# Splitting the squared keys for the norm: ScalarE squares twice and VectorE subtracts, instead of a ScalarE copy and a GpSimd subtraction

## The chip, the cores and the metric

The kernel runs on one core of one Trainium2 chip. The metric is the device time of one execution in microseconds (us), shown as the median of several runs. The profile's times are also in us; durations of single instructions are given in ns or us. The engines are TensorE (PE; its weight loads are listed as PEld), VectorE (DVE), ScalarE (ACT), GpSimd (POOL) and SyncE (SP), which issues nearly all DMAs. Each engine works through its own list of instructions in order.

## The reference

One layer of a hybrid trunk over 1024 tokens and 1024 channels: an input projection, an RWKV-7 branch and an HGRN2 branch, a gated merge, cross-attention into 256 memory tokens, a SwiGLU feed-forward, and a last RMSNorm. What the change touches is the normalisation of the RWKV-7 keys: each head (64 channels) of `k * k_k` is divided by its length.

```python
cols = cols + mu * (token_shift(cols) - cols)          # cols = rmsnorm(x) @ w_in
r, k, v, w_lo, a_lo, g_lo = jnp.split(cols, RW_SPLITS, axis=-1)
...
kk = heads(k * k_k)
kk = kk * lax.rsqrt(jnp.maximum(jnp.sum(kk * kk, axis=-1, keepdims=True), 1e-24))
k_mod = heads(k * (1 + (a - 1) * k_a))
```

## The kernel before

All matrix products of this stage run in a rounded float32 format (F32R). Where the full precision of float32 is wanted, an operand is split into `hi`, the value rounded to F32R, and `lo`, the remainder `src - hi`, also in F32R. Products are then sums over the parts: `mm3` adds three matmuls (hi·hi, hi·lo, lo·hi). The helper `split` makes the two parts: by default ScalarE copies `src` to `hi` (L283), then GpSimd subtracts (L287).

The stage around the change is `rw_prep`, from about 30 to 375 us of the span. It works feature-major: a tile `j` is 128 of the 1024 channels, and each tile has two halves `h` of 512 tokens. For each `j` it projects three columns of `w_in`, in the order k, r, v, each for both halves: 24 matmuls of 128x512 into a PSUM tile `pproj` (8 blocks of the contraction, three matmuls each). `shifted` then mixes each result with the one of the token before (ScalarE writes `mshift` at L439, VectorE finishes `k`, `r` or `v` at L442). The weights come as two DMAs of 256 KB per column (`wraw`); each half is split into `whi` (ScalarE) and `wlo` (GpSimd for the first half, VectorE for the second).

`factors(j, h)` is the rest, a generator that the loop steps between the projections. Its chain for one half is:

- ScalarE squares the scaled keys into `sq` (L510); `split` makes `sqh` and `sql` from it (L511, seen in the profile as L283 and L287).
- PE makes two products `pza` (L518, L519), ScalarE their sigmoids `sg` and `aa`, VectorE the running sum `cum` (L522), ScalarE the exponentials `E` and `En`.
- PE sums the squares over each head: two matmuls `pq` with the block matrix `hsum`, first on `sqh`, then on `sql` (L533).
- VectorE takes the maximum and the reciprocal of `pq` into `d` (L535, L536), and makes `ka` (L541), the products `AR` (L545) and `BK` (L555, L557, two of each, 64 rows at a time) and `rb` (L561). GpSimd makes another part of `AR` (L542), `t` (L549) and `km` (L550, L551).
- PE sums `rb` per head into `pb` (L565) and transposes `v` into `pv` (L570); VectorE copies `pb` to `bon` (L567) and makes `VZ` (L577), GpSimd adds a bias to it (L579). DMAs store `ar_d`, `bk_d`, `v_d` and `z_d`.

The order on each engine isn't written out in the code. The tile framework schedules this stage when the kernel is built, by costs and priorities of its own, so a change of one instruction moves others on every engine's list. The framework also adds the waits. The planner `Pace`, which the next stage uses, takes no part here.

Of the kernel before, what the change touches and what calls it, by code (L numbers as in the profile page):

```python
# [10 lines left out]
F32 = mybir.dt.float32  # L11
F32R = mybir.dt.float32r
AF = mybir.ActivationFunctionType
ALU = mybir.AluOpType
# [170 lines left out]
def tile_trunk(ctx, tc, x, mem, norm_mix_g, w_in, rw_mu, rw_w0, rw_w2, rw_a0, rw_a2, rw_g2,  # L185
# [3 lines left out]
    nc = tc.nc  # L189
# [76 lines left out]
    def vc(name, i=0):  # L266
        if name == "mix":
            return GM[:, i:i + 1]
        return VC[:, VI[name] + i:VI[name] + i + 1]
# [10 lines left out]
    def split(hi, lo, src, hi_eng="act", lo_eng="pool"):  # L280

        if hi_eng == "act":
            nc.scalar.activation(hi, src, AF.Copy)  # L283
        else:
            nc.vector.tensor_copy(hi, src)
        e = nc.gpsimd if lo_eng == "pool" else nc.vector
        e.tensor_tensor(lo, src, hi.bitcast(F32), op=ALU.subtract)  # L287
# [136 lines left out]
    def rw_prep(rctx):  # L424
# [79 lines left out]
        def factors(j, h):  # L504
            (ks, rs, vs), w2h, w2l, lnb = tiles[j]
            sl = slice(h * HALF, (h + 1) * HALF)
            k, r, v = ks[h], rs[h], vs[h]
            T = lambda name: fp.tile([P, HALF], F32, tag="tmp", name=name, bufs=10)
            sq = T("sq")
            nc.scalar.activation(sq, k, AF.Square, scale=vc("kk", j))  # L510
            sqs = [fp.tile([P, HALF], F32R, tag="tmp", name=n, bufs=10) for n in ("sqh", "sql")]  # L511
            split(*sqs, sq)

            sg, aa = T("sg"), T("aa")
            for n, (dst, bias) in enumerate(((sg, "w0"), (aa, "a0"))):
# [122 lines left out]
        for j in range(D // P):  # L638
            if j:
                inputs = tile_inputs(j)  # L640
                next(inputs)
            last()
            next(inputs)
            last()
            for h in range(NHALF):
                f = factors(j, h)
                next(f)
                next(inputs)
                with tc.issue_after(next(f)):
                    next(consts, None)  # L650
                next(inputs)
                pending.append(f)
# [1680 lines left out]
```

## Time and profile before

| | |
|---|---|
| median of 3 runs | 2314.49 us (2312.69 to 2317.57) |
| profiled execution | 2314.19 us, its span 2312.5 us |
| PE busy | 2269.3 us (98%) |
| DVE busy | 1575.7 us (68%) |
| ACT busy | 1142.2 us (49%) |
| POOL busy | 1061.6 us (46%) |
| mean granted TensorE clock | 0.996 |

The span runs from the first to the last instruction; the profiled execution is 1.7 us longer than that. A view by windows gives for each stretch the busy time of each engine with the number of instructions in brackets, the granted clock of TensorE (1.00 is full speed), the busy share of the DMA engines and their GB/s. A view in order of time gives for each row the start, the duration, the engine, the line, the operation, output<-inputs, the shape, the count, and in square brackets the idle time before the row with what ended it. Ends of matmuls are modelled and overlap: in a row of 128x512 matmuls each is shown with 0.39 us, while they start every 0.227 us.

### The profile page before, as it was taken

Reading aid. Unit: us, or ns where it says so; the run is one execution under the profiler, and the core shown is the slowest. Engines: PE = TensorE matmul, PEld = TensorE weight load, DVE = VectorE, ACT = ScalarE, POOL = GpSimd, SP = SyncE. Lnnn points to the kernel's source line nnn. Section 1 sums busy time; section 2 is a strip of 40 time slices with the busy share of each in tenths; the row PEclk is TensorE's granted clock in tenths of the full one; section 3 lists DMA queues with packets and bytes.
Section 4 is the critical chain, followed back from the end, with each engine's and each line's share of the span. In section 5 each row is a group of like instructions: output and inputs, shape, how many; then the busy total and the mean of one; then the engine's idle time right before and its main releaser. Section 6 shows DMA issues by size and latency. Waiting matters only on the chain.

```text
span 2312.5 us, 47099 instructions
## 1 busy us (share of the span) xinstructions
PE 2269.3 (98%) x18262; PEld 1863.3 (81%) x18262; DVE 1575.7 (68%) x2513; ACT 1142.2 (49%) x2275; POOL 1061.6 (46%) x1145
## 2 busy tenths in 40 slices
PE   7999999999999999999999999999999999999998
PEld 5788887777888887888788888888888888888887
DVE  5888984666777657777666566655778665566655
ACT  6546464556565655654666424443552333334433
POOL 3656664555565555666566200000266655551212
PEclk9999999999999999999999999999999999999999
DMA  5444555343334244534334897117933423348653
GB/s 174 113 127 121 136 131 165 72 104 76 87 108 126 75 117 108 141 83 112 89 89 129 277 355 259 60 56 256 289 125 119 131 91 115 96 160 308 201 172 120
DMA packets 393691, 327.94 MB, mean 142 GB/s; under 512 B 107595, under 2 KB 318653, under 8 KB 392061
## 3 DMA queue, kind: packets, MB, share of 16 engines
q1 hardware_dynamic: 391549, 319.17, 45.6%
q0 software_dynamic: 1344, 4.72, 0.5%
q8 instruction: 144, 2.36, 0.4%
q10 hardware_dynamic: 576, 1.05, 0.1%
q14 instruction: 78, 0.64, 0.1%
HBM read 228.12 MB, written 96.21 MB: 140 GB/s over the span
## 4 chain that ended last, share of the span: by engine, by line
PE 72%; DVE 4%; DMA 3%; issue 2%; ACT 1%; POOL 1%; SPq 0%; ACTq 0%; POOLq 0%; DVEq 0%
PE pproj L103 22%; PE P L302 6%; PE P L303 6%; PE P L301 6%; PE pw L303 3%; PE pw L302 2%; PE pw L301 2%; PE cm L103 2%; PE psA L103 2%; PE psc L103 1%; PE po L103 1%; PE acc L302 1%; PE pq L303 1%; PE pq L302 1%; PE pq L301 1%
## 5 line engine op out<-in xcount | busy, mean ns | idle before, releaser
L103 PE MATMUL pproj<-uh,whi 128*128 128x512 f32 x768 | 320.1, 417 | 1.2 <-DVE q L103 0.7
L103 PE MATMUL pproj<-uh,wlo 128*128 128x512 f32 x768 | 300.9, 392 | 2.9 <-POOL wlo L103 2.3
L103 PE MATMUL pproj<-ul,whi 128*128 128x512 f32 x768 | 301.4, 392 | 0.0
L287 POOL TENSOR_TENSOR wl<-wraw,wh 128x512 fp32r<-128x512 f32 x87 | 122.4, 1416 | 201.2 <-ACT wh L283 153.6
L103 POOL TENSOR_TENSOR wlo<-wraw,whi 128x512 fp32r<-128x512 f32 x96 | 128.9, 1354 | 122.1 <-ACT whi L103 116.5
L301 PE MATMUL pproj<-uh,whi 128*128 128x512 f32 (+1 forms) x432 | 172.2, 399 | 0.9 <-ACT uh L329 0.7
L303 PE MATMUL pproj<-uh,wlo 128*128 128x512 f32 (+1 forms) x432 | 170.8, 395 | 2.0 <-POOL wlo L287 2.0
L103 PEld LDWEIGHTS pproj<-uh,whi 128*128 128x128 f32 x768 | 144.5, 188 | 34.0 <-DVE q L103 2.0
L302 PE MATMUL pproj<-ul,whi 128*128 128x512 f32 (+1 forms) x432 | 171.0, 396 | 0.0
L103 PEld LDWEIGHTS pproj<-ul,whi 128*128 128x128 f32 x768 | 144.4, 188 | 32.3
L283 ACT ACTIVATE whi<-wraw 128x512 fp32r<-128x512 f32 (+1 forms) x166 | 101.6, 617 | 136.4 <-PE pw L303 71.5
L103 PEld LDWEIGHTS pproj<-uh,wlo 128*128 128x128 f32 x768 | 145.0, 189 | 28.7 <-POOL wlo L103 2.7
L278 POOL TENSOR_TENSOR ss<-ss,nhalf 128x4 f32<-128x4 f32 (+1 forms) x7 | 6.2, 881 | 322.9 <-DMA wraw<-in_xa_wo_dram 186.7
L287 POOL TENSOR_TENSOR wlT<-wraw,whT 128x512 fp32r<-128x512 f32 x72 | 103.1, 1440 | 81.3 <-ACT whT L283 58.9
L287 DVE TENSOR_TENSOR wlo<-wraw,whi 128x512 fp32r<-128x512 f32 x134 | 93.1, 700 | 55.1 <-ACT whi L283 53.1
L283 ACT ACTIVATE wh<-wraw 128x512 fp32r<-128x512 f32 x143 | 86.9, 623 | 88.4 <-PE P L302 65.5
L103 ACT ACT_TABLE_LOAD x90 | 115.5, 1283 | 13.5 <-DVE m L103 6.4
L302 PE MATMUL acc<-wl,th 128*128 128x512 f32 x308 | 119.9, 389 | 0.2 <-DVE wl L287 0.2
L301 PE MATMUL acc<-wh,th 128*128 128x512 f32 x308 | 119.8, 389 | 0.0
L303 PE MATMUL acc<-wh,tl 128*128 128x512 f32 x308 | 119.8, 389 | 0.0
L2277 DVE TENSOR_TENSOR tl<-tl,th 128x512 fp32r<-128x512 f32 x77 | 60.1, 795 | 62.6 <-ACT th L2276 61.3
L301 PE MATMUL pw<-whi,ah 128*128 128x512 f32 x256 | 100.7, 393 | 0.9 <-ACT ah L283 0.6
(461 smaller groups left out, 6436.3 us busy)
## 6 DMA issues: line engine op xcount, KB each, us to landing
wraw<-in_w_in_dram SPq DMA_DIRECT2D x148, 256.0 KB
wraw<-in_ffn_w_dram SPq DMA_DIRECT2D x145, 256.0 KB
y<-in_ffn_w_dram SPq DMA_DIRECT2D x22, 512.0 KB
wsum_d<-y SPq DMA_DIRECT2D x11, 1024.0 KB
hsum_d<-s SPq DMA_DIRECT2D x44, 256.0 KB
tl<-hsum_d SPq DMA_DIRECT2D x44, 256.0 KB
wraw<-wsum_d SPq DMA_DIRECT2D x44, 256.0 KB
hid_d<-s SPq DMA_DIRECT2D x33, 256.0 KB
```

The source lines that it names most:

```text
L103: r = getattr(self.engine, op)(*a, **kw)
L278: nc.gpsimd.tensor_tensor(dst, tmp, nhalf[:, 0:n], op=ALU.pow)
L283: nc.scalar.activation(hi, src, AF.Copy)
L287: e.tensor_tensor(lo, src, hi.bitcast(F32), op=ALU.subtract)
L301: nc.tensor.matmul(ps, ah, bh, start=first, stop=False)
L302: nc.tensor.matmul(ps, ah, bl, start=False, stop=False)
L303: nc.tensor.matmul(ps, al, bh, start=False, stop=last)
L2277: tt(hl, hl.bitcast(F32), hh.bitcast(F32), op=ALU.subtract)
```

## The change

`sqh` no longer is a copy of `sq`: ScalarE squares the scaled keys a second time, straight into the F32R tile. The remainder `sql` is subtracted on VectorE instead of GpSimd. Per half this is one ScalarE instruction in place of another, one instruction less on GpSimd and one more on VectorE; there are 16 halves.

```diff
@@ -509,7 +509,8 @@
             sq = T("sq")
             nc.scalar.activation(sq, k, AF.Square, scale=vc("kk", j))
             sqs = [fp.tile([P, HALF], F32R, tag="tmp", name=n, bufs=10) for n in ("sqh", "sql")]
-            split(*sqs, sq)
+            nc.scalar.activation(sqs[0], k, AF.Square, scale=vc("kk", j))
+            nc.vector.tensor_tensor(sqs[1], sq, sqs[0].bitcast(F32), op=ALU.subtract)
```

Since the diff adds a line, lines from L512 on have a number higher by one in the changed kernel. The scheduler gives other orders in `rw_prep`. The first place is VectorE in a tile of the middle, j = 5 (j = 2 to 6 read alike here): the second half of the work of h = 0 up to `d` of h = 1 (`d_2612`). Before:

```order
L557 TENSOR_TENSOR BK<-km,En 64x8x64
L561 SCALAR_TENSOR_TENSOR rb<-r,VC,km 128x512
L442 SCALAR_TENSOR_TENSOR r<-pproj,VD,mshift 128x512
L522 SCALAR_TENSOR_TENSOR cum<-rst_120,sg 128x512
L287 TENSOR_TENSOR wlo<-wraw,whi 128x512
L535 TENSOR_SCALAR d_2612<-pq 128x512
```

Now:

```order
L558 TENSOR_TENSOR BK<-km,En 64x8x64
L562 SCALAR_TENSOR_TENSOR rb<-r,VC,km 128x512
L442 SCALAR_TENSOR_TENSOR r<-pproj,VD,mshift 128x512
L513 TENSOR_TENSOR sql<-sq,sqh 128x512
L287 TENSOR_TENSOR wlo<-wraw,whi 128x512
L523 SCALAR_TENSOR_TENSOR cum<-rst_120,sg 128x512
L442 SCALAR_TENSOR_TENSOR v<-pproj,VD,mshift 128x512
L536 TENSOR_SCALAR d_2612<-pq 128x512
```

`sql` of h = 1 stands behind `rb` of h = 0 and `r` of h = 1; `cum` and `wlo` have changed places, and a `v` has moved ahead of `d` (before, it stood behind the reciprocal that follows `d`, and a second `v` behind the next `rb`, where there is none now).

The second place is GpSimd at the end of h = 1 of the same tile and the start of the next, where `sql` of the next tile's h = 0 stood. Before:

```order
L579 TENSOR_TENSOR VZ<-VZ,lnb 128x512
L287 TENSOR_TENSOR sql<-sq,sqh 128x512
L287 TENSOR_TENSOR wlo<-wraw,whi 128x512
L579 TENSOR_TENSOR VZ<-VZ,lnb 128x512
L528 COPY eLall<-E 128x8
```

Now:

```order
L580 TENSOR_TENSOR VZ<-VZ,lnb 128x512
L287 TENSOR_TENSOR wlo<-wraw,whi 128x512
L580 TENSOR_TENSOR VZ<-VZ,lnb 128x512
L529 COPY eLall<-E 128x8
```

Only `sql` is gone there; in the half h = 0 it is gone from between `km` and the memset of `E` in the same way.

The third place is VectorE where that `sql` went, at the start of the next tile (j = 6, h = 0). Now:

```order
L568 COPY bon<-pb 128x8
L578 TENSOR_TENSOR VZ<-pv,bon 128x512
L513 TENSOR_TENSOR sql<-sq,sqh 128x512
L568 COPY bon<-pb 128x8
L442 SCALAR_TENSOR_TENSOR k<-pproj,VD,mshift 128x512
```

It stands between the `VZ` of h = 0 and the `bon` of h = 1; the rows around it are as before. On PE the two matmuls `pq` stand at the same place as before, one behind the other, in every half but the second of the first tile: there nine matmuls of a projection now stand between the one on `sqh` and the one on `sql`.

Three more moves are small. In the last tile VectorE's subtraction for `g2s` (L673) has moved from ahead of `ka` of h = 0 to behind `sql` of h = 1, and GpSimd's for `g2l` from ahead of its part of `AR` (L542) to behind it. On ScalarE in the tiles 2 to 6 the second `whi` of a column has moved ahead of the table load for `sg`, and a `mshift` ahead of the one for `E`. On SP the first of two weight loads at a tile's end has moved behind the stores `v_d` and `z_d` of h = 1.

## The prediction

> **What bounds the kernel.** I read the page first, then the waits of TensorE in the stage that the change touches, then that stage in order of time, engine by engine.
>
> ```profile
> PE 2269.3 (98%) x18262; PEld 1863.3 (81%) x18262; DVE 1575.7 (68%) x2513; ACT 1142.2 (49%) x2275; POOL 1061.6 (46%) x1145
> 50.00:375.00 325.00, 317.02 (x1464) 261.61 (x1464) 278.18 (x291) 174.82 (x263) 197.82 (x265) 0.98 0.48 130
> ```
>
> The first row is the page's busy times, the second the window of the stage: PE is busy for 317.0 of 325 us, so PE sets the time there too, and an instruction on another engine costs only where PE waits for it. VectorE is the next engine: 278.2 of 325 us (86%), against 198 on GpSimd and 175 on ScalarE. The change puts work on the fuller of the two engines. What PE waited for between 40 and 375 us (total, times, longest):
>
> ```profile
> PE pb L565 <- DVE bon L567: 3.0, 3, 1.4
> PE pq L533 <- POOL sql L287: 2.9, 1, 2.9
> ...
> PE pv L570 <- DVE v L442: 0.5, 1, 0.5
> ```
>
> So before the change `sql` makes PE wait once, in the first tile, for 2.9 us. In the other 15 halves it is early. The question is whether it is early on VectorE.
>
> **The prices of the instructions.** Groups of one shape in the stage (count, busy us, mean ns):
>
> ```profile
> L287 POOL TENSOR_TENSOR sql<-sq,sqh 128x512 fp32r<-128x512 f32 x16 | 21.8, 1361 | 0.5 <-POOL low L287 0.4
> L287 DVE TENSOR_TENSOR wlo<-wraw,whi 128x512 fp32r<-128x512 f32 x23 | 15.8, 687 | 0.0
> L510 ACT ACTIVATE sq<-k,VC 128x512 f32<-128x512 f32 x16 | 11.5, 717 | 33.4 <-DVE k L442 33.4
> L283 ACT ACTIVATE sqh<-sq 128x512 fp32r<-128x512 f32 x16 | 10.0, 626 | 0.3
> ```
>
> GpSimd loses 16 x 1.36 = 21.8 us. VectorE gains 16 subtractions; the same subtraction of the same shape, `wlo`, takes 0.69 us there, so 11.0 us. ScalarE pays 16 x (0.717 - 0.626) = 1.5 us. None of these three sums lies on the path by itself: ScalarE waits 33.4 us for `k` ahead of the same squares, and that idle time covers the 1.5 us. SP's moved weight load leaves only behind three small stores that were behind it, and its reader on ScalarE has its turn about a quarter of a tile later; if that cover is gone, `whi` is late and with it a projection. I cost both at nothing.
>
> **Where the new instruction is late.** PE in tile 5 (start, duration): the second `pq` of h = 0 and that of h = 1:
>
> ```profile
> 259.01 0.39 PE L533 MATMUL pq<-sql,hsum 128*128 128x512 f32 x1
> ...
> 271.29 0.39 PE L533 MATMUL pq<-sql,hsum 128*128 128x512 f32 x1
> ```
>
> Between the two halves PE has 12.28 us of work that waits for nothing. On VectorE the chain of h = 0 starts with the first of these and must reach `sql` of h = 1 by the last, since `sql` now stands behind `rb` and `r`:
>
> ```profile
> 259.44 0.69 DVE L535 TENSOR_SCALAR d<-pq 128x512 f32<-128x512 f32 x1 [0.89 <-PE pq L533]
> ...
> 264.85 1.78 DVE L555 SCALAR_TENSOR_TENSOR BK<-k,VC,t 64x512 f32<-64x512 f32 x1
> 266.55 2.56 DVE L545 TENSOR_TENSOR AR<-ka,E 64x512 f32<-64x512 f32 x2
> 269.14 0.68 DVE L557 TENSOR_TENSOR BK<-km,En 64x512 f32<-64x512 f32 x1
> 269.84 1.69 DVE L555 SCALAR_TENSOR_TENSOR BK<-k,VC,t 64x512 f32<-64x512 f32 x1
> 271.46 0.95 DVE L557 TENSOR_TENSOR BK<-km,En 64x512 f32<-64x512 f32 x1
> 272.44 0.84 DVE L561 SCALAR_TENSOR_TENSOR rb<-r,VC,km 128x512 f32<-128x512 f32 x1
> 273.20 0.74 DVE L442 SCALAR_TENSOR_TENSOR r<-pproj,VD,mshift 128x512 f32<-128x512 f32 x1
> 273.87 1.21 DVE L522 TENSOR_TENSOR_SCAN cum<-rst,sg 128x512 f32<-128x512 bf16 x1
> ```
>
> The rows left out are `r`, the reciprocal and `ka`. VectorE is never idle in it; from the first `pq` it is a chain of 15 us. In the old times `sql` would start where `cum` does, at 273.87, and end at 273.87 + 0.69 = 274.56, which is 3.27 us after PE asked for it. (The old `sql` was done on GpSimd at 266.57 + 1.28 = 267.85, the first row of the next fence.) PE works in order, so behind the waiting `pq` stand the 24 matmuls of `v` and all that follows.
>
> Part of the lateness goes with the change itself. GpSimd at the same time:
>
> ```profile
> 266.57 1.28 POOL L287 TENSOR_TENSOR sql<-sq,sqh 128x512 fp32r<-128x512 f32 x1
> 269.17 0.12 POOL L524 MEMSET E<- 128x8 f32 x1 [1.33 <-DVE AR L545]
> 269.27 1.72 POOL L287 TENSOR_TENSOR wlo<-wraw,whi 128x512 fp32r<-128x512 f32 x1
> 270.95 1.78 POOL L485 TENSOR_TENSOR w2l<-w2r,w2h 64x128 fp32r<-64x128 f32 x2
> ```
>
> and VectorE in the half h = 1, where GpSimd is silent:
>
> ```profile
> 283.29 1.40 DVE L545 TENSOR_TENSOR AR<-ka,E 64x512 f32<-64x512 f32 x2
> ...
> 285.42 0.75 DVE L555 SCALAR_TENSOR_TENSOR BK<-k,VC,t 64x512 f32<-64x512 f32 x1
> ```
>
> The pair L545 takes 1.40 us there and 2.56 beside the old `sql`: the two engines' subtractions and products exclude each other, and the one that comes second waits. With `sql` gone the pair ends 1.16 us earlier. But GpSimd's memset of `E` waits for that pair, and behind it stand `wlo` and `w2l`, whose inputs are there; they come earlier too and again hold up L555 (1.69 against 0.75 in the last row), L557 and `rb`. Played through with these durations, and each instruction held until the other engine's ends, `rb` ends near 272.3 instead of 273.28, so 0.95 of the 1.16 us is kept. I take a wait of 3.27 - 0.95 = 2.3 us. Bounds: with nothing kept 3.3; with all of 1.16 kept and the two later collisions (0.94 for L555, 0.26 + 0.09 for L557 and `rb`) gone as well, 3.27 - 2.45 = 0.8. I take 2.3 as nearest to the rows, since nothing removes `wlo`. Tiles 1 to 6 have the same PE distance and nearly the same chain, so 6 x 2.3 = 13.8 us.
>
> `sql` of h = 0 has its turn while VectorE waits for `mshift` and `sg`, well ahead of its `pq`: nothing. In the first tile `sql` of h = 1 falls behind `rb`. That wait is there already (2.9 us), and PE now does nine matmuls of it first; by the same collisions I make it 0.3 us longer in all.
>
> The last tile has its own rows:
>
> ```profile
> 342.26 0.77 DVE L673 TENSOR_TENSOR g2s<-g2r,g2s 32x512 fp32r<-32x512 f32 x1
> 352.32 1.21 DVE L522 TENSOR_TENSOR_SCAN cum<-rst,sg 128x512 f32<-128x512 bf16 x1
> ...
> 347.91 0.39 PE L533 MATMUL pq<-sql,hsum 128*128 128x512 f32 x1
> ```
>
> There `sql` would end at 352.32 + 0.69 = 353.0, 5.1 us after PE's turn. L673 (0.77) has moved behind it, and GpSimd's window loses `sql` (1.74 there) but gains `g2l` (1.30): 5.1 - 0.8 - 0.4 = 3.9 us. Bounds 4.3 and, with all of 1.74 kept, 2.6.
>
> **The clock after a wait.** What a wait of 1 to 3 us does to TensorE's granted clock (the column ahead of the last two):
>
> ```profile
> 134.49 1.05 PE L565 MATMUL pb<-hsum,rb 128*128 128x2 f32 x8 [1.30 <-DVE bon L567]
> 75.00:76.50 1.50, 1.50 (x4) 1.21 (x5) 1.49 (x3) 0.00 (x0) 1.44 (x4) 0.50 0.77 175
> 134.50:139.50 5.00, 5.00 (x21) 4.24 (x22) 2.31 (x5) 4.94 (x8) 4.22 (x5) 0.66 0.52 126
> 370.00:375.00 5.00, 4.37 (x12) 2.55 (x11) 1.22 (x2) 2.23 (x4) 4.02 (x5) 0.52 0.83 192
> 463.66 1.00 PE L103 MATMUL cm<-Z,AR 128*64 128x64 f32 x15 [1.66 <-DVE Z L103]
> 463.00:465.00 2.00, 1.29 (x32) 1.15 (x32) 1.79 (x6) 1.42 (x6) 1.32 (x3) 1.00 0.30 33
> ```
>
> After the waits of 2.9, 1.3 and 1.4 us the clock fell to half; after 1.66 us at 463 it did not. In the second window 5.0 x 0.34 / 0.5 = 3.4 us ran at half speed, which loses 1.7 us. I take three in four, so 1.28 us for each new wait: 7 x 1.28 = 9.0 us. [...]
>
> **What goes away.** PE comes to `pb` later, so VectorE's `bon` is ready: 3.0 us of waits, and the 0.5 for `v`, which now stands earlier. Of the `bon` waits two (1.30 and 1.44) were followed by half clock, 2 x 1.7 = 3.4. Together 6.9 us, at the ends of tiles 1, 5 and 7.
>
> **The sum.** 13.8 + 3.9 + 0.3 + 9.0 - 6.9 = +20.1 us. Against the profiled execution's 2314.2 that is 2334.3; the median of the runs is 0.3 above the profiled one, so 2334.6, and I say 2335. (A difference of 0.2%, 4.6 us, is about what a measurement of this kernel tells from none.)
>
> **Rivals.**
> 1. The waits come, but the clock stays up behind them, as it did at 463 us: 20.1 - 9.0 = +11.1, 2325.6. For it: that one wait. Against it: the other three. [...]
> 2. The waits are small, 0.8 us. That needs `wlo` and `w2l` to miss VectorE's gaps. Then 6 x 0.8 + 2.6 + 0.3 - 6.9, and a lost clock in the last tile alone, 1.3: +2.1, 2316.6, no difference. For it: all of `sql`'s 1.16 us comes back. Against it: the rows of `wlo` and `w2l`, which only come earlier.
> 3. Faster: freed of GpSimd, the chain fits between the two `pq`. From `pq` at 259.01 to the end of a `sql` it is 274.56 - 259.01 = 15.55 us; without any collision 1.03 less for the first L555 and 2.45 less for the rest, 12.07, under PE's 12.28. It decides from 3.27 us saved. Then only the removals count, with 0.8 left in the last tile: 0.3 + 0.8 - 6.9 = -5.8, 2308.7. Against it: the first L555 (1.78) meets GpSimd's `km`, not `sql`, and that stays.
>
> **How the numbers follow.** Forecast 0.57, rival 1 0.23, rival 2 0.14, rival 3 0.06. The predicted time is the forecast's, 2335. With nothing kept of the 1.16, seven drops of 1.7 us and 4.3 in the last tile it is 19.6 + 4.3 + 0.3 + 11.9 - 6.9 = +29.2, 2343.7: the upper end is 2344. At the lower end I leave out rival 3 and about the lower half of rival 2: 2317. The forecast and rival 1, with the upper part of rival 2, are slower by over 0.2%: 0.82; within: 0.12; faster: 0.06.
>
> **What would show it.** In the waits of PE: `pq` on VectorE's `sql`, eight times, some 2.3 us each in tiles 1 to 6 and 4 in the last, where there was one on GpSimd; the waits of `pb` on `bon` gone; windows of half clock behind most of the new waits; the pair L545 of h = 0 at 1.40 us; the distance from tile to tile up from 38.3 to some 41.5 us; the time from 375 us on unchanged. I am wrong if `sql` of h = 1 ends by the time of its `pq`, if the clock holds at 1.00 behind waits of 2 us, or if the time is given back after the stage.

## The result and the profile after

The changed kernel takes 2333.71 us (median of 5 runs, 2331.25 to 2335.66), the kernel before 2313.85 us in the runs beside it. The ratio is 1.0083, with a 95% interval of 1.0069 to 1.0098: 19.9 us slower. The prediction said 2335. The profiled execution of the changed kernel took 2335.24 us, with a span of 2333.2.

In the changed kernel `sql` is L513, `pq` L534, `AR` L546 and `rb` L562. What PE waited for between 40 and 400 us (total, times, longest), and the window of the stage in the same form as before (PE, its weight loads, VectorE, ScalarE, GpSimd; then granted clock, DMA share, GB/s):

```profile
PE pq L534 <- DVE sql L513: 19.1, 8, 3.5
...
50.00:375.00 325.00, 304.62 (x1381) 250.60 (x1380) 275.34 (x293) 167.55 (x246) 177.71 (x233) 0.97 0.45 122
```

One wait on GpSimd's `sql` has become eight on VectorE's. The waits on `bon` and `v` are gone; the two rows left out are waits for other tiles, at the start of the stage. PE is busy 12.4 us less in the same 325 us, although VectorE is no fuller than it was (275.3 us for 278.2; the same window now holds some 16 us less of the stage's work). That points to the place of the instruction rather than to VectorE's total, and the experiments test it. The eight waits, tile by tile (start, duration, and in brackets the idle time ahead):

```profile
77.87 0.50 PE L534 MATMUL pq<-sql,hsum 128*128 128x512 f32 x1 [3.21 <-DVE sql L513]
119.24 0.50 PE L534 MATMUL pq<-sql,hsum 128*128 128x512 f32 x1 [3.35 <-DVE sql L513]
161.05 0.51 PE L534 MATMUL pq<-sql,hsum 128*128 128x512 f32 x1 [1.88 <-DVE sql L513]
201.32 0.54 PE L534 MATMUL pq<-sql,hsum 128*128 128x512 f32 x1 [1.88 <-DVE sql L513]
243.16 0.50 PE L534 MATMUL pq<-sql,hsum 128*128 128x512 f32 x1 [1.88 <-DVE sql L513]
283.40 0.66 PE L534 MATMUL pq<-sql,hsum 128*128 128x512 f32 x1 [1.88 <-DVE sql L513]
324.91 0.50 PE L534 MATMUL pq<-sql,hsum 128*128 128x512 f32 x1 [1.53 <-DVE sql L513]
366.81 0.79 PE L534 MATMUL pq<-sql,hsum 128*128 128x512 f32 x1 [3.51 <-DVE sql L513]
```

VectorE in tile 5, from the `pq` of h = 0 to the `sql` of h = 1, and GpSimd's `wlo` beside it:

```profile
269.51 0.69 DVE L536 TENSOR_SCALAR d<-pq 128x512 f32<-128x512 f32 x1 [2.15 <-PE pq L534]
...
276.53 1.40 DVE L546 TENSOR_TENSOR AR<-ka,E 64x512 f32<-64x512 f32 x2
277.95 0.68 DVE L558 TENSOR_TENSOR BK<-km,En 64x512 f32<-64x512 f32 x1
278.65 1.69 DVE L556 SCALAR_TENSOR_TENSOR BK<-k,VC,t 64x512 f32<-64x512 f32 x1
280.26 0.95 DVE L558 TENSOR_TENSOR BK<-km,En 64x512 f32<-64x512 f32 x1
281.25 0.84 DVE L562 SCALAR_TENSOR_TENSOR rb<-r,VC,km 128x512 f32<-128x512 f32 x1
...
282.67 0.68 DVE L513 TENSOR_TENSOR sql<-sq,sqh 128x512 fp32r<-128x512 f32 x1
278.16 1.63 POOL L287 TENSOR_TENSOR wlo<-wraw,whi 128x512 fp32r<-128x512 f32 x1
```

`sql` ends at 283.35, and PE goes on at 283.40. The pair of `AR` is at 1.40 us, as forecast, and what follows it has the lengths it had before (1.69, 0.95, 0.84), only earlier. The granted clock (the column ahead of the last two) in the 5 us behind the four equal waits of tiles 2 to 5:

```profile
161.00:166.00 5.00, 4.95 (x22) 1.00 0.54 143
201.30:206.30 5.00, 4.98 (x15) 0.66 0.54 142
243.10:248.10 5.00, 4.94 (x22) 1.00 0.53 143
283.40:288.40 5.00, 5.00 (x15) 0.66 0.43 113
```

Two of the four were followed by half clock. What that costs can be read from the starts above: 201.32 - 161.05 = 40.27 and 283.40 - 243.16 = 40.24 us without, 243.16 - 201.32 = 41.84 us with it, so 1.6 us each. (In the kernel before, these steps from tile 2 to tile 5 took 38.2 to 38.3 us.) Half clock followed also in tiles 0, 1 and 7 (0.66, 0.66 and 0.50), and not in tile 6.

Where the loss stands along the span: starts of the same PE instructions after, less before, in us (median of those within 25 us from the time given in the kernel before, for the first profile of the changed kernel, its second profile (e10) and the experiments e2, e5, e7 and e8 below):

```
from    changed  again    e2     e5     e7     e8
 160      4.7     4.3    5.1    5.8    4.9   -2.1
 280     13.4    11.3   13.9   12.9   10.4   -2.8
 400     16.3    13.3   17.4   16.8    9.9   -5.2
 880     19.0    16.7   20.9   19.5   13.9   -5.0
1680     17.5    16.5   20.0   17.3   22.1   -4.2
2240     21.2    20.2   19.5   17.1   22.7   -3.7
```

So 16.3 of the 21.2 us of this execution were lost in the stage that was changed, and some 5 behind it. Most of these 5 come between 1680 and 2240 us, at one wait for `hB` at the start of the feed-forward part, with half clock behind it (0.50 from 1727.42 to 1730.82); the kernel before waits 0.5 us for `hB`:

```profile
1727.07 0.52 PE L301 MATMUL P<-hB,wh 128*128 128x512 f32 x1 [2.76 <-ACT hB L2026]
```

### The profile page after: what moved, and what is told of

It is laid out like the page before. It is cut to its first block, busy times and chain, and to the rows that moved or that the text cites. A ratio compares the mean times of both kernels' runs of the same rounds, so it can differ in the third digit from the quotient of the medians.

```text
span 2333.2 us, 47083 instructions
## 1 busy us (share of the span) xinstructions
PE 2274.2 (97%) x18262; PEld 1866.8 (80%) x18262; DVE 1582.6 (68%) x2529; ACT 1144.7 (49%) x2275; POOL 1055.9 (45%) x1129
## 4 chain that ended last, share of the span: by engine, by line
PE 76%; DVE 3%; DMA 2%; POOL 1%; issue 1%; ACT 1%; SPq 0%; ACTq 0%; POOLq 0%; DVEq 0%
PE pproj L103 21%; PE P L302 6%; PE P L303 6%; PE P L301 6%; PE acc L303 3%; PE acc L302 3%; PE acc L301 3%; PE pw L303 2%; PE pw L302 2%; PE pw L301 2%; PE cm L103 2%; PE psA L103 2%; PE psc L103 1%; PE po L103 1%; PE pq L303 1%; PE pq L302 1%
```

## Experiments: which part of the change costs

The theory: `sql` of h = 1 is late because it stands behind `rb` and `r` on VectorE. Rival A: the second Square on ScalarE is at fault. Rival B: VectorE is simply fuller, and each of the 16 subtractions costs the same. Four kernels take the change apart.

**e1, the ScalarE part alone.** Kernel before, with

```diff
-            split(*sqs, sq)
+            nc.scalar.activation(sqs[0], k, AF.Square, scale=vc("kk", j))
+            nc.gpsimd.tensor_tensor(sqs[1], sq, sqs[0].bitcast(F32), op=ALU.subtract)
```

> The ScalarE part of the change alone: `sqh` comes from a second Square, `sql` stays on GpSimd. Theory (the loss comes from where `sql` of h = 1 stands in VectorE's order, behind `rb` and `r`): as the kernel before, 2314 us, 2311 to 2317; PE waits at `pq` for GpSimd's `sql` in the first tile alone (about 2.9 us), and for `bon` three times (3.0 us). Rival A (the second Square: 0.72 us for 0.63, read from `k`, on ScalarE, makes `sqh` and what stands behind it late): slower, by up to the whole 20 us.

Measured: 2315.23 us, ratio to the kernel before 1.0005 (0.9996 to 1.0014). The stage's waits are those of before:

```profile
PE pb L566 <- DVE bon L568: 3.0, 3, 1.4
PE pq L534 <- POOL sql L513: 2.9, 1, 2.9
```

**e2, the VectorE part alone.** `split(*sqs, sq, lo_eng="dve")`: the copy on ScalarE stays, the subtraction goes to VectorE.

> The VectorE part of the change alone: `sqh` stays a copy of `sq` on ScalarE, `sql` comes from VectorE in both halves. Theory: as the changed kernel, 2334 us, 2330 to 2337, with eight waits of `pq` on VectorE's `sql`, 1.5 to 3.5 us each, 19 us together, and the waits on `bon` gone. Rival A (the second Square is at fault): back at 2314.

Measured: 2332.63 us, 1.0079 (1.0065 to 1.0093), with the eight waits:

```profile
PE pq L533 <- DVE sql L287: 20.0, 8, 4.5
```

The two parts are thus told apart: all of the loss is with the subtraction's engine, none with the Square. Rival A is out.

**e3 and e5, one half each.** The change, but in e3 with the first, in e5 with the second of these lines:

```diff
+            (nc.gpsimd if h else nc.vector).tensor_tensor(sqs[1], sq, sqs[0].bitcast(F32), op=ALU.subtract)
+            (nc.vector if h else nc.gpsimd).tensor_tensor(sqs[1], sq, sqs[0].bitcast(F32), op=ALU.subtract)
```

> As the change, but `sql` of h = 1 stays on GpSimd, and only that of h = 0 goes to VectorE. Theory: that of h = 0 has its turn well ahead of its `pq` and costs nothing; 2314 us, 2309 to 2318, no wait of `pq` on VectorE, the pair of `AR` on VectorE in h = 0 still at 2.5 us. Rival B (VectorE is simply fuller: each of the 16 subtractions costs the same): half of the loss, 2324.

> The other half: `sql` of h = 1 goes to VectorE, that of h = 0 stays on GpSimd. Theory: the whole loss, 2333 us, 2328 to 2337, with a wait of `pq` on VectorE's `sql` in each of the eight tiles, about 1.9 us in tiles 1 to 6 and over 3 in the first and the last. Rival B: half of the loss, 2324.

Measured: e3 2314.07 us, 0.9999 (0.9987 to 1.0011); e5 2332.89 us, 1.0082 (1.0068 to 1.0095). The waits of PE on `sql`, and the pair of `AR` in h = 0 of tile 5, e3 first:

```profile
PE pq L534 <- POOL sql L513: 2.9, 1, 2.9
265.42 2.56 DVE L546 TENSOR_TENSOR AR<-ka,E 64x512 f32<-64x512 f32 x2
```

```profile
PE pq L534 <- DVE sql L513: 20.0, 8, 4.5
277.71 1.40 DVE L546 TENSOR_TENSOR AR<-ka,E 64x512 f32<-64x512 f32 x2
```

The eight subtractions of h = 0 cost nothing on VectorE, the eight of h = 1 all of it. Rival B is out. In e5 the pair is as short as in the changed kernel, so the relief comes from the `sql` of h = 1 that GpSimd no longer does.

## Experiments: the place in VectorE's order

**e4d** gives `sql` alone a higher priority when the order is built; **e4a** gives it to `sq`, `sqh` and `sql`. In both, `sql` of h = 1 stands on VectorE among the products of h = 0, beside `AR` and ahead of three of the four `BK`, of `rb` and of `r`.

```diff
+            with tc.high_priority(100):
+                nc.vector.tensor_tensor(sqs[1], sq, sqs[0].bitcast(F32), op=ALU.subtract)
```

> The whole change, with a higher priority for `sql` alone: in h = 1 it now stands on VectorE right behind the products `AR` of h = 0, ahead of `BK`, `rb` and `r`, some 4 us earlier. Theory (the place in VectorE's order is the cause, not the engine): `sql` is ready about 2 us before its `pq`, no waits on it but in the first tile, and with GpSimd's copy of the work gone the pair of `AR` at 1.40 us: 2305 to 2316 us, I say 2311. Rival (VectorE has too little room; the chain behind `sql`, now 0.69 us later, makes PE wait at `pb` or in the next projection instead): 2320 to 2330, with waits on `bon`, `r` or `VZ`.

> As the run before, but with the priority on all three instructions (`sq`, `sqh` and `sql`), which also moves some projections of PE past the `pza` matmuls. Theory: the same as that run, 2305 to 2316, I say 2311; if the two differ by more than 5 us, the moved order on ScalarE and PE matters and not `sql` alone.

Measured: e4d 2314.60 us, 1.0000 (0.9992 to 1.0009); e4a 2312.48 us, 0.9988 (0.9980 to 0.9997). VectorE in tile 5 of e4a, and then PE's turn at that `sql`:

```profile
265.14 0.68 DVE L547 TENSOR_TENSOR AR<-ka,E 64x512 f32<-64x512 f32 x1
265.74 0.68 DVE L514 TENSOR_TENSOR sql<-sq,sqh 128x512 fp32r<-128x512 f32 x1
269.96 0.39 PE L535 MATMUL pq<-sql,hsum 128*128 128x512 f32 x1
PE pb L567 <- DVE bon L569: 4.2, 3, 2.0
PE pq L535 <- DVE sql L514: 0.6, 1, 0.6
```

`sql` ends at 266.42, 3.5 us before its turn; PE doesn't wait, and the loss is gone with the work still on VectorE. That is the mechanism: the same instruction on the same engine costs some 19 us behind `rb` and nothing ahead of it. e4d moves `sql` alone and e4a other instructions too, and both lose nothing, so it is the place of `sql` that counts. The gain that I expected over the kernel before came only in part (1.6 us in the medians for e4a, none for e4d). In e4a the waits on `bon` are back, 4.2 us for 3.0. In e4d the stage did end 3.7 us ahead of the kernel before, and 3.7 us were lost between 1680 and 2240 us, where PE waits 2.6 us for `hB`.

## Experiments: the sizes of the two disputed terms

**e6, the collision put back.** The prediction let the shorter pair of `AR` give back a part of its gain to GpSimd's `wlo` and `w2l`. Here GpSimd does the subtraction too, early, and VectorE does it again:

```diff
+            if h:
+                nc.gpsimd.tensor_tensor(sqs[1], sq, sqs[0].bitcast(F32), op=ALU.subtract)
             nc.vector.tensor_tensor(sqs[1], sq, sqs[0].bitcast(F32), op=ALU.subtract)
```

> The change, and in h = 1 GpSimd still does the same subtraction into the same tile first, early; VectorE then does it again in its place. So the collision of GpSimd with the pair of `AR` is back, and nothing else. Theory A (all that the pair gained without the collision, 1.2 us, shortened the waits): pair at 2.5 us, waits of `pq` up from 1.9 to 3.0 us in tiles 1 to 6, together 7 us more, 2338 to 2346. Theory B (as in the prediction's sum: `wlo` and `w2l` come earlier with the shorter pair and take back a part): waits up by less than 1 us, 2335 to 2339.

Measured: 2349.42 us, 1.0151 (1.0138 to 1.0164). The pair, the instruction after next, the wait and the granted clock of e6:

```profile
287.94 2.57 DVE L548 TENSOR_TENSOR AR<-ka,E 64x512 f32<-64x512 f32 x2
291.24 1.70 DVE L558 SCALAR_TENSOR_TENSOR BK<-k,VC,t 64x512 f32<-64x512 f32 x1
207.48 0.79 PE L536 MATMUL pq<-sql,hsum 128*128 128x512 f32 x1 [3.05 <-DVE sql L515]
251.68 0.79 PE L536 MATMUL pq<-sql,hsum 128*128 128x512 f32 x1 [3.05 <-DVE sql L515]
207.50:212.50 5.00, 5.00 (x12) 0.50 0.51 139
```

The pair is 1.17 us longer (2.57 for 1.40) and the wait too (3.05 for 1.88). Theory A holds: each instruction behind the pair keeps its length, early or late, and all of the relief reaches PE. The time of e6 is 3.4 us above the range of theory A. All four of its waits in tiles 2 to 5 were followed by half clock, three of them through the whole 5 us behind (0.50; 0.72 in tile 5): a tile without half clock would take 40.26 - 1.88 + 3.05 = 41.4 us, and from 207.48 to 251.68 it took 44.2, so 2.8 us lost where the shorter waits of the changed kernel lost 1.6.

**e7 and e7b, the waits filled.** To take the half clock away and leave the lateness, PE gets four matmuls more ahead of `pq` in h = 1 (e7b: in tiles 1 to 5 alone):

```diff
+            for _ in range(4 * h):
+                nc.tensor.matmul(ps, hsumr, sqs[0], start=True, stop=True)
```

> The change, with four more matmuls of 0.39 us on PE ahead of the pair of `pq` in h = 1 (`sqh` once more into the same bank, overwritten by the pair), so that PE is busy for 1.57 us of each wait. Nothing else is sped up: what follows still starts when `sql` is there. Theory (four of the seven new waits cost a stretch of half clock on top of themselves, 1.7 us each): waits of 0.3 us in tiles 1 to 5, no half clock behind them, 2327 to 2331 us. Rival (the half clock after a wait costs nothing, since the end of the tile is set elsewhere, or it falls without an idle PE too): 2333 to 2336.

> The four extra matmuls in tiles 1 to 5 alone (20 on PE, not 32). In the run with 32 the stage ended 6.4 us sooner than in the changed kernel, and 10 us were lost again between 900 and 1260 us, by waits that the profile puts down to no engine. Theory (the half clock behind the waits costs the stage its share; the later loss hangs on where the added instructions push PE's program, not on the waits): again no half clock in tiles 2 to 5, the stage some 4 us shorter than in the changed kernel, and the time 2327 to 2331 if the later waits are gone. Rival (a shorter stage is given back later in any case): 2333 to 2338, with the same waits between 900 and 1260 us.

Measured: e7 2336.58 us, 1.0097 (1.0082 to 1.0112); e7b 2335.36 us, 1.0094 (1.0079 to 1.0109). The extra matmuls and a filled wait in e7, and the granted clock behind the waits of tiles 3 and 5:

```profile
279.79 1.09 PE L534 MATMUL pq<-sqh,hsum 128*128 128x512 f32 x4
282.06 0.51 PE L536 MATMUL pq<-sql,hsum 128*128 128x512 f32 x1 [0.95 <-DVE sql L513]
201.60:206.60 5.00, 5.00 (x22) 1.00 0.54 140
282.00:287.00 5.00, 4.94 (x22) 1.00 0.43 117
```

The fill was smaller than I worked out: matmuls overlap, and four took 0.93 us of the wait, not 1.57. It was enough. The granted clock was 1.00 over the 5 us behind the waits of tiles 3 to 5 of e7 and 2 to 5 of e7b, from wait to wait of tiles 2 to 5 it is 40.2 to 40.3 us in both, and at 400 us e7 stood 6.4 us ahead of the changed kernel, as the theory says. But the time doesn't show it: e7's median is above both ranges that were named ahead. In the table above e7 loses 12 us between 400 and 1680, where its code is that of the changed kernel, a good part of it in stretches like this one (wait ahead of a matmul of the mixing, and the granted clock):

```profile
920.96 0.63 PE L103 MATMUL py<-TT,BS 32*32 32x32 f32 x28 [1.14 <-issue]
920.00:940.00 20.00, 19.04 (x260) 0.91 0.26 75
```

"issue" means that the profile shows nothing that PE waited for. In e7b a similar loss, 8.5 us, came at other places; 2.7 us of it are a wait for ScalarE's `whi` at 1362 us. So e7b's theory on the later loss fell: it did not go away with 20 added instructions in place of 32. What makes it is open. Such waits need no longer list on PE: e9 below, which adds no matmul, has two of some 1 us as well. Inside the stage the half clock is shown to cost what was read from the tile distances; the total of these two runs is no evidence on it.

**e10, the changed kernel unaltered**, for a second profile.

> The changed kernel once more, unaltered, for a second profile. In its first profile the four equal waits of 1.88 us halved the clock in tiles 3 and 5 and not in 2 and 4, and a wait of 2.8 us on `hB` at the FFN's start made the profile 3.7 us longer, which two other kernels with the same stage did not have. Theory A (the moment at which a wait falls decides on the clock, and it differs from one execution to the next): the waits of 1.88 us come again to the hundredth, half clock behind other ones of them; Theory B (the program decides): the same tiles again. For the wait on `hB`: under 1 us if it belonged to that one execution, 2.8 us again if it is the changed kernel's own.

Measured: 2334.05 us. The wait of tile 5 again, and the granted clock behind the waits of tiles 3, 4 and 5:

```profile
282.98 0.51 PE L534 MATMUL pq<-sql,hsum 128*128 128x512 f32 x1 [1.88 <-DVE sql L513]
201.30:206.30 5.00, 5.00 (x17) 0.69 0.48 128
243.10:248.10 5.00, 5.00 (x24) 1.00 0.47 128
283.40:288.40 5.00, 5.00 (x24) 1.00 0.36 100
```

The wait of tile 5 is the same to the hundredth, and this time the clock held. The same program with the same wait can go either way: theory A. (In e5 it was tiles 2 and 4 that fell, 0.66 over 5 us, and 3 and 5 that held, 1.00.) Which way it went follows a pattern in the traces, shown in the last section. The wait on `hB` came again, at 2.6 us for 2.8, so it belongs to the changed kernel and not to one execution; e4d and e6 have it too (2.6 and 2.7), e2 and e5, whose waits on `sql` are like those of the changed kernel, have none above 0.5, and what sets it stays open.

## Experiments: a version that beats both

In e4a the waits on `bon` were most of what was left of the stage's stalls. **e8** is e4a with `bon` on ScalarE; **e9** is the kernel before with that one line:

```diff
-            nc.vector.tensor_copy(bon, pb.rearrange("p i q -> p (i q)"))
+            nc.scalar.activation(bon, pb.rearrange("p i q -> p (i q)"), AF.Copy)
```

> The priority on all three instructions, and besides the copy `bon` goes from VectorE to ScalarE, which is idle there. Theory (in that kernel the waits of `pb` on `bon`, 4.2 us in tiles 0, 1 and 7, and the half clock behind them, 3 x 1.7 us, are all that is left of the stage's stalls): waits on `bon` gone, 2303 to 2308 us, ahead of the kernel before and of the changed one. Rival (what waits for `bon` is then late elsewhere, as `VZ` or `wlo` on VectorE and GpSimd): 2309 to 2315.

> The kernel before with that one move alone: `bon` on ScalarE. It tells what in the run beside it comes from `sql` and what from `bon`. Theory: waits on `bon` gone (3.0 us and two stretches of half clock, 3.4), the first tile's wait for GpSimd's `sql` stays: 2306 to 2311 us, 2 to 4 us behind the run beside it. Rival: no change, 2312 to 2316.

Measured: e8 2309.75 us, 0.9979 (0.9970 to 0.9988); e9 2316.44 us, 1.0012 (1.0004 to 1.0021). PE's waits, e8 first:

```profile
PE pv L572 <- DVE VZ L579: 2.1, 2, 1.4
```

```profile
PE pv L570 <- DVE VZ L577: 2.1, 4, 1.0
```

In both, `bon` is early and PE then waits for `VZ`, which VectorE makes from it: 2.1 us in place of the 4.2 (e4a) and 3.0 us (kernel before) for `bon`. So e8 came out in the rival's range and not in the theory's. Alone the move is worth nothing: e9 is 0.1% slower, above both ranges. Together with the early `sql` it is some 5 us below the kernel before, the fastest of the kernels run, and its profile has that lead by the end of the stage: 5.2 us at 400 us.

## Why the prediction was right, point by point

The mechanism was the one that it gave, and the experiments show it: the subtraction on VectorE (e2), in h = 1 (e3, e5), behind `rb` and `r` (e4a, e4d). The sum was 20.1 us, and 21 us came in the profiled execution, 19.9 in the medians. That it came so near is in part luck, for the terms did not all have their size:

| term | predicted | in the profile |
|---|---|---|
| waits of tiles 1 to 6 | 13.8 | 3.35 + 4 x 1.88 + 1.53 = 12.4 |
| wait of the last tile | 3.9 | 3.5 |
| wait of the first tile, longer by | 0.3 | 3.21 - 2.89 = 0.3 |
| half clock behind new waits | 9.0 | 4 of 7, 4 x 1.6 = 6.4 |
| removed | -6.9 | `bon` and `v` 3.5, two half clocks 3.2: -6.7 |
| behind the stage | 0 | 21.2 - 16.3 = 4.9 |

- **The waits of tiles 2 to 6.** The mis-sized step is "0.95 of the 1.16 us is kept". All of it is kept (e6), which gives 3.27 - 1.17 = 2.1 us. The profile's 1.88 (tiles 2 to 5; it is 1.53 in tile 6, which stays unexplained) is counted from the modelled end of the matmul ahead; that matmul started at 281.13, and in the kernel before `pq` on `sql` started 0.24 us behind it. From 281.37 to 283.40 it is 2.03 us. The distance of tiles agrees: 40.25 us without half clock for 38.3 before. Tile 1 is another case than I said, and "nearly the same chain" doesn't hold for it: its wait is 3.35 us, the pair of `AR` gained nothing there (1.79 us for 1.70), and VectorE stood idle for GpSimd's `km`:

```profile
113.70 0.83 DVE L558 TENSOR_TENSOR BK<-km,En 64x512 f32<-64x512 f32 x1 [1.20 <-POOL km L552]
```

- **The clock.** The step "three in four" gave 1.28 us for each wait. A half clock costs 1.6 us, and 4 of 7 came in this execution. Of the twelve waits of 1.88 us in the changed kernel's two profiles and e5, five were followed by half clock, so the chance was too high. The last tile ran at half clock for about twice as long both before and after (0.52 and 0.50 over 5 us); the table prices it at 1.6 us on both sides, which leaves the balance nearly the same. That the new waits cost clock at all holds: behind waits of 1.88 us it fell to 0.50. Rival 1 (2325.6) fails on this.
- **Rival 2** (waits of 0.8 us) and **rival 3** (the chain fits) fail on the eight waits. Rival 3 was right in one thing: once `sql` stands elsewhere, there is room for it on VectorE (e4a).
- **"The time from 375 us on unchanged"** was wrong. Some 5 us were added there in the first profile, 7 in the second, 0.3 in e5, in the first mostly by the wait on `hB`. That and the terms that were too big nearly cancel by chance; the stage by itself lost 16.3 us, not 20.1. The total was nearer than its parts.

## What to carry to other kernels

When an instruction moves to another engine, price the queue that it lands in, not its own duration: 0.68 us of work made PE wait 1.5 to 3.5 us a tile because it stood behind a chain that ended after its reader's turn, and cost nothing when it stood six instructions earlier (e4a). Look for the half that has slack: the same move was free for h = 0, where VectorE waits for others anyway. If such a move costs, change the order before giving up the move.

## What the runs showed of the hardware

- The same wait was followed by half clock in one execution and not in the next. In the changed kernel and e10 the wait of 1.88 us of tile 5 was once followed by a granted clock of 0.66 over 5 us and once by 1.00.
- The traces show a pattern that goes with it. Between 60 and 2280 us of the kernel before and of the changed one, the granted clock is 0.50 in stretches of 3.41 us (nine) and of 6.83 us (two), and 1.00 elsewhere; here are the changes around those of tiles 3 and 5 of the changed kernel:

```profile
201.20:201.66 0.46, 0.34 (x1) 1.00 0.74 167
201.67:205.07 3.40, 3.40 (x10) 0.50 0.65 172
283.59:286.99 3.40, 3.40 (x9) 0.50 0.58 154
```

  These two stretches start 81.92 us apart, which is 24 times 3.413, and in each of the two traces all stretches start a whole number of times 3.413 us apart. Counted in steps of 3.413 us from the starts in its own trace, each of the eight waits of 1.88 us in the changed kernel's two profiles began so far into its step (us), and half clock followed or not:

```
tile       2           3           4           5
changed    1.89 no     1.20 half   2.08 no     1.36 half
e10        2.11 no     1.42 half   2.28 no     1.58 no
```

  The three that began by 1.42, and so ended within the step, were followed by half clock from the step's end on; the five that ran over the end were not. A wait of 2.31 us that was cut by a step's end into 1.19 and 1.12 (changed kernel, from 429.16 us) was not followed by it either; one of 2.31 us within a step (kernel before, from 412.81 us) was. Of PE's waits of more than 1.2 us in the traces of these two kernels between 60 and 2280 us, all 8 with 1.88 us or more in one step were followed by half clock; of the 8 that have less in each step, 3. This is read from the traces; no run moved a wait on purpose to test it.
- Longer waits lost more: 1.6 us behind 1.88, and in e6 some 2.8 us behind 3.05 in the tiles 2 to 4, where the half clock lasted through the 5 us behind the wait (0.50).
- Where VectorE was freed of the collision in h = 0 it met another one in h = 1: the pair of `AR` there takes 2.77 us in the changed kernel for 1.40 before. GpSimd makes `km` in that time (295.84 to 297.42). PE doesn't wait for it.

```profile
295.19 2.77 DVE L546 TENSOR_TENSOR AR<-ka,E 64x512 f32<-64x512 f32 x2
```
